# High parts ahead of low ones, P5's sum on P1's weight tile, and a new order of the last product, in a decoder trunk on one core

## The chip, the core and the metric

The kernel runs on one core of one Trainium2 chip. A core has five engines with a queue each, executed in order: TensorE (PE, matmuls), VectorE (DVE), ScalarE (ACT), GpSimd (POOL) and SyncE (SP). SP here only issues loads; POOL issues the loads that add to what lies in a tile. Data come from the chip's memory into on-chip tiles; products are accumulated in PSUM banks and read from there by DVE and ACT. The metric is the device time of one execution in microseconds (us).

## The reference

A trunk of two layers on 512 tokens of width 1024, all in float32. Layer 0 mixes tokens with a gated linear recurrence, layer 1 with a spatial gate; each mixer stands between two feed-forward blocks of width 2816 that count half.

```python
def swiglu(x, w_in, w_out):
    g, u = jnp.split(x @ w_in, 2, axis=-1)
    return (jax.nn.silu(g) * u) @ w_out
...
    for i in range(DEPTH):
        h = h + 0.5 * swiglu(rms_norm(h, ffn1_norm[i]), ffn1_w_in[i], ffn1_w_out[i])
        hn = rms_norm(h, mix_norm[i])
        ...
        h = h + m          # m: recurrent mixer (i = 0) or spatial gating mixer (i = 1)
        h = h + 0.5 * swiglu(rms_norm(h, ffn2_norm[i]), ffn2_w_in[i], ffn2_w_out[i])
    return rms_norm(h, final_norm)
```

## The kernel before

**Products.** A float32 operand is split into a high part (rounded, by ACT, line 96) and a low part (the rest, by DVE, line 87 or 93); a product is three matmuls, left high by weight high, left low by weight high, left high by weight low (lines 362 to 364). The splits of weights are called whi and wlo, those of activations hi and lo.

**Seven products instead of eight.** `seven` cuts both operands of a matrix product into 2 x 2 blocks and forms it from seven products, P1 P2 P5 P6 P3 P7 Q4, by the scheme of Strassen and Winograd. Their left operands are blocks or sums of blocks of the activations (A11, A12, S1, S2, S4, S3, A22, in that order); S1 = A21 - A22, S2 = S1 - A11, S4 = S2 + A12 and S3 = -S2 - A22. Their right operands are weight blocks: B11 for P1, B21 for P2, B11 + B12 for P5, B11 + B12 + B22 for P6, the same and B21 for Q4, B22 for P3, and B12 + B22 for P7 (signs left aside). P1, P6, P7 and Q4 gather in bank pair A (Q4 of an out product in Q), P5 and P3 in C, P2 in B. Each product is cut into two parts, ci = 0 and 1, by rows of the weights. A product's `posts` read its bank when its second part is through: in an out product they add the bank to the trunk X (`upd`, line 93 by its helper, "x<-A" in the profile), where P6's must have read bank A before P7 writes it again.

**Steps.** All products stand in one list `subs`, 550 entries, one for a product's part; an entry's twelve or so matmuls are one step. The loop at the end of `trunk` goes through them in order and emits for step i: waiting accumulating loads that are due (`run_pending`); hooks "pre"; the split of the weights of step i + 3 (`Sub.split`) after the DVE sum of the next one (`Sub.add`); hooks "mid" and "rest"; plain loads into weight tiles that are free (`load_more`, SP's queue); the matmuls; hooks "end"; the product's posts; hooks "late". Each engine executes its instructions in this order. There are 8 weight tiles as loaded ("raw") and 4 each of whi and wlo.

**Sums of weight blocks** are made in three ways. `Raw(plus=...)` loads one block plainly, and two steps later issues a load on POOL's queue that adds the second (line 136; `pending`). `Sub.then` issues such an adding load right after a split has read the tile. `Sub.tile` has DVE add two tiles (line 87, "raw<-raw,raw"), and `tile_then` then adds a further block to the second tile. A seven with `own=True` loads B11 a second time for P5 and gives P5 and P7 sums of the first kind; with `own=False`, P5's sum is one of DVE's, and P7 goes on with the tile of that sum. P6 adds B22 by DVE and then B21 by a load for Q4. Where P6 comes four steps or more behind P5 (`far`: the recurrent mixer's out product, and part 0 of the spatial one's), P5's split is followed by the load of B22 instead.

**Stages.** A feed-forward block is three times a group of columns of w_in and the matching rows of w_out: first a "pair" of column tiles by plain products (`pair_plain`, line 727) and a chunk of four tiles by `seven` (`chunk`), then two such chunks twice (lines of `FF_PARTS`); each time the out product follows (`out_blocks`, own=True). Chunks have own=False, but one of the spatial mixer is own. The recurrent out product has the order P1 P5 P2 for each part, P6 P3 for each, then P7 and Q4; its left operands are split `lead` = 2 steps ahead. The last out product has an order of its own, `FinalNorm.ORDER`, and its P3 is held back to the end with both parts together (`joined`).

**Turning activations.** A left operand's blocks are transposed by PE into a PSUM bank (`Group.turn`, line 264, "e"), from which ACT and DVE take them, split or as they are (`Group.take`, `Group.direct`). `direct` runs in the opening, where the first norm's blocks are turned, and at the norms between blocks (`BlockNorm`). In the opening the first pair's own turns (`left_blocks`, from `post` in `pair_plain`) stand at a lag of 4 steps. The first chunk takes bank pair B from the two `aux` banks, in which the turned blocks also lie; its P2's post adds B to c (line 87, "c<-c,B"). ACT squares the quarters of X there for the next norm (`squares`).

Of the kernel before, what the change touches and what calls it, by code (L numbers as in the profile page):

```python
# [13 lines left out]
P = 128  # L14
# [38 lines left out]
def trunk(ctx: ExitStack, tc: tile.TileContext, a: dict, out: bass.AP):  # L53
# [57 lines left out]
    class Raw:  # L111
# [1 line left out]

        halves = False

        def __init__(self, src, shape, plus=None):
            self.src, self.shape, self.plus, self.uses, self.done = src, shape, plus, 0, 0

        def turn(self):
            self.uses += 1  # L120
# [2 lines left out]
        def load(self):  # L123
            _, k, c = self.shape
            t = rawp.tile([P, 1024], F32, tag="raw", name=nm("raw"))
            self.v = t[:, : k * c].rearrange("p (k c) -> p k c", k=k)
            live.add(self)
            self.fetch()
            if self.plus is not None:
                pending.append((now[0] + 2, self))  # L130

        def fetch(self):
            nc.sync.dma_start(out=self.v, in_=self.src)
# [68 lines left out]

    raws = []

    def raw_of(src, shape, plus=None):
        raws.append(Raw(src, shape, plus))
        return raws[-1]

    subs = []
# [35 lines left out]
    class Group:  # L245
# [39 lines left out]
        def direct(self, name, ps, gains):  # L285

            hi, lo = self.hl[name] = slot(F32R, "hi")[:, : self.n * H], slot(F32R, "lo")[:, : self.n * H]
            for q, g in enumerate(gains):
                c = slice(q * H, (q + 1) * H)
                act(hi[:, c], ps[:, c], AF.Copy, scale=g)  # L290
                stt(lo[:, c], ps[:, c], g, f32(hi[:, c]), ALU.mult, ALU.subtract)

        def stage(self, n, name, src, gains=None, parts=True, where=None, direct=0):
# [40 lines left out]
    def seven(block, cuts, left, w, posts, order=None, own=False, apart=False, joined=None, spare=bank):  # L334

        bk, raw, held = {}, {}, []
        banks = dict(BANK, Q4=("Q", True)) if apart else BANK

        def mm_of(prod, ci):
            name, fresh = banks[prod]
            pairs = cuts[ci]

            def mm(sub):
                if fresh and ci == 0:
                    for s in range(2):  # L350
                        bk[name, s] = (spare if name == "B" else bank)(name)[:, :w]
                if prod == joined and ci == 0:
                    held.extend((sub, q, i) for q, i in enumerate(pairs))
                    return
                for s in range(2):
                    ps = bk[name, s]
                    k = {} if fresh else dict(skip_group_check=True)
                    for sb, q, i in (held if prod == joined else []) + [(sub, q, i) for q, i in enumerate(pairs)]:
                        zh, zl = left(prod, i, s)
                        wh, wl = sb.hi[:, q, :], sb.lo[:, q, :]  # L360
                        end = i == cuts[-1][-1]
                        nc.tensor.matmul(ps, zh, wh, start=fresh and i == 0, stop=False, **k)  # L362
                        nc.tensor.matmul(ps, zl, wh, start=False, stop=False, **k)  # L363
                        nc.tensor.matmul(ps, zh, wl, start=False, stop=end, **k)  # L364
                    if ci == len(cuts) - 1 and prod in posts:
                        posts[prod](s, ps)
            return mm

        order = order or [(p, ci) for p in ORDER for ci in range(len(cuts))]

        def far(ci):
            return own and order.index(("P6", ci)) - order.index(("P5", ci)) >= 4

        for prod, ci in order:
            def new(k, n, plus=None):
                b = lambda k, n: block(k, n, cuts[ci])
                return raw_of(b(k, n), [P, len(cuts[ci]), w], plus and b(*plus))

            tile = then = tile_then = None
            if prod == "P1":  # L380
                r = raw[11, ci] = new(0, 0)
            elif prod == "P2":
                r = new(1, 0)
            elif prod == "P5":
                if own:
                    raw[11, ci] = new(0, 0, (0, 1))
                    if far(ci):
                        then = block(1, 1, cuts[ci])
                else:
                    tile = raw[12, ci] = new(0, 1)  # L390
                    tile_then = block(1, 1, cuts[ci])
                r = raw[11, ci]
            elif prod == "P6" and far(ci):
                r, then = raw[11, ci], block(1, 0, cuts[ci])
            elif prod == "P6":
                r, tile, then = raw[11, ci], new(1, 1), block(1, 0, cuts[ci])
                raw[22, ci] = tile
            elif prod == "P3":
                r = new(1, 1) if far(ci) else raw[22, ci]
            elif prod == "P7":  # L400
                r = new(0, 1, (1, 1)) if own else raw[12, ci]
            else:
                r = raw[11, ci]
            subs.append(Sub(r, mm_of(prod, ci), None, tile, then, tile_then))
        return order

# [149 lines left out]
                hook(n + 4, "pre", lambda: self.take(1))  # L556


    def out_blocks(w, k0, groups, scale, norm=None, order=None, own=False):

        n = [g for g in groups]
        cuts, bases, i, r = [], {}, 0, k0
# [57 lines left out]
        for i, (prod, ci) in enumerate(order):  # L620
            if prod in ("P3", "P6", "P7", "Q4"):
                lead = 6 if ends and prod == "P3" else 4 if isinstance(norm, TileNorm) and prod in ("P7", "Q4") else 3 if 1 in n else 2
                hook(at0 + i - lead, "mid", lambda ci=ci, name=LEFT[prod]: gs[ci].parts(name))
        return gs

# [27 lines left out]
        return left_of(lambda: S.z)  # L653


    def chunk(w_in, f0, nt, group, spare=bank):

        w = nt * P
        c1, c2, c3, c5, ht = {}, {}, {}, {}, {}

        def rt(t):
            return S.rt[:, t : t + 1]

        def new(d, s, name):
            d[s] = slot(name=name)[:, :w]
            return d[s]

        def p1(s, ps):
            act(new(c1, s, "c1"), ps, AF.Copy)

        def p2(s, ps):
            tt(c1[s], c1[s], ps, ALU.add)
            hook(now[0] + 1, "mid", lambda: act(c1[s], c1[s], AF.Silu, scale=rt(s)))

        def p5(s, ps):
            act(new(c5, s, "c5"), ps, AF.Copy)

        def p6(s, ps):
            act(new(c2, s, "c2"), ps, AF.Copy)

        def p3(s, ps):
            tt(c2[s], ps, c2[s], ALU.subtract)
            stt(c2[s], c2[s], rt(s), c1[s], ALU.mult, ALU.mult)
            ht[s] = c2[s]
            if s == 1:
                left_blocks(group, ht, 0)

        def p7(s, ps):
            act(new(c3, s, "c3"), ps, AF.Copy)
            hook(now[0] + 1, "mid", lambda: tt(c5[s], c5[s], c3[s], ALU.subtract))  # L690

        def q4(s, ps):
            s4 = slot(name="s4")[:, :w]
            act(s4, ps, AF.Silu, scale=rt(2 + s))
            stt(c5[s], c5[s], rt(2 + s), s4, ALU.mult, ALU.mult)
            ht[2 + s] = c5[s]
            if s == 1:
                left_blocks(group, ht, 1)

        seven(in_block(w_in, lambda n: n * DFF + f0 * P, w), [[0, 1], [2, 3]], x_left(), w,  # L700
              dict(P1=p1, P2=p2, P5=p5, P6=p6, P3=p3, P7=p7, Q4=q4), spare=spare)

    def pair_plain(w_in, f0, group, first=False):

# [31 lines left out]
        def post(half):  # L736
            for s in range(2):
                ps, t = st[half, s], 2 * half + s
                if t not in ht:
                    silu(half, s)  # L740
                o = slot(name="h")[:, :w]
                stt(o, ps[:, w:], S.rt[:, t : t + 1], ht[t], ALU.mult, ALU.mult)
                ht[t] = o
            left_blocks(group, ht, half, 4 if first else 2)

        at0 = len(subs)
        for i, (half, left) in enumerate(((0, "A12"), (0, "A11"), (1, "A22"), (1, "A21"))):
# [27 lines left out]
    def ffn(w_in, w_out, norm):  # L775
        f0 = 0
        for i, sizes in enumerate(FF_PARTS):
            groups, p0 = [], f0
            for n in sizes:
# [3 lines left out]
                    f0 += 2  # L783
                else:
                    groups.append(Group(n // 2))
                    chunk(w_in, f0, n, groups[-1], aux if len(subs) == 8 else bank)
                    f0 += n
            gs = out_blocks(w_out, p0, [g.n for g in groups], 0.5, norm if i == len(FF_PARTS) - 1 else None, own=True)
            gs.update(enumerate(groups))
# [2 lines left out]
    class FinalNorm:  # L792

        ORDER = [(p, ci) for p in ("P1", "P2", "P5", "P6", "P7", "Q4", "P3") for ci in range(2)]

        def __init__(self):
            self.gain, self.q, self.m, self.s = {}, {}, {}, {}
# [95 lines left out]
    def recurrent(w_in, w_out, norm):  # L895
# [132 lines left out]
        for i, at in enumerate(((11, 12, 15), (13, 14, 16))):  # L1028
            for fn, n in zip((groups[i].s2, groups[i].s4, groups[i].s3), at):
                hook(y0 + n, "pre", fn)  # L1030

        def y_post(c, ps):
            ym[c] = ps
# [31 lines left out]
        order = [(p, ci) for ci in range(2) for p in ("P1", "P5", "P2")]  # L1065
        order += [(p, ci) for ci in range(2) for p in ("P6", "P3")]
        order += [(p, ci) for p in ("P7", "Q4") for ci in range(2)]
        gs = out_blocks(w_out, 0, [2, 2], 1.0, norm, order, own=True)
        gs.update(enumerate(groups))


# [358 lines left out]
                         (4, "rest", lambda: (value(0, "A21"), value(1, "A21")))):  # L1430
        hook(n, phase, fn)
    squares(4, "rest", "A11")
    squares(4, "rest", "A12")
    squares(5, "rest", "A22")
    squares(5, "rest", "A21")
    rstd(6, (0, "rest"), (0, "rest"), (1, "pre"))
    first.rest(1, None)
    hook(20, "end", vec_rest_t)
# [50 lines left out]
```

## Time and profile before

| what | value |
|---|---|
| median of 3 runs | 1652.9 us (1652.57 to 1654.43) |
| the profiled execution | 1653.5 us |
| its span in the trace | 1651.7 us |
| matmuls (PE) | 7475 |
| granted TensorE clock, mean | 0.995 |
| moved by plain loads (q1) and by POOL's (q0) | 182.74 MB and 87.63 MB |
| their share of the 16 DMA engines' span | 35.8% and 31.7% |

The span runs from the first instruction to the last in the trace; 1.8 us of the profiled execution lie outside it. A group in the profile is named by line, engine, operation and tiles, with tile numbers left out: "A<-whi,hi" is a matmul into a bank called A from a weight's high part and an activation's high part. A wait names the instruction that came last before the waiting one could start. The page's list of DMA issues gives for each kind of load its bytes and its median time from issue to landing: the plain 512 KB loads of w_out take 5.4 us in the median, those of w_in 4.5.

### The profile page before, as it was taken

To read this page: it belongs to the slowest core of one execution; us is meant where nothing else is said; L and a number is where in the kernel's file an instruction comes from. 1 tells how busy PE (TensorE), PEld (TensorE's weight loads), DVE (VectorE), ACT (ScalarE), POOL (GpSimd) and SP (SyncE) were. 2 spreads that over 40 slices of the span, in tenths; PEclk is the share of its full clock that TensorE was granted. 3 is DMA by queue.
4 is the path that set the end of the run, shared out by engine and by line. 5 is a ranking of instruction groups with operands and counts; after the bars stand their busy time and mean duration, and the time that the engine had idled before them with its cause. 6 is when DMAs were issued, how large, how long until landed. Compare 5 with 4: busy or idle time off the path is not lost.

```text
span 1651.7 us, 20816 instructions
## 1 busy us (share of the span) xinstructions
PE 1621.3 (98%) x7475; PEld 1334.7 (81%) x7475; DVE 1361.2 (82%) x1821; ACT 1033.6 (63%) x1501; POOL 214.1 (13%) x194
## 2 busy tenths in 40 slices
PE   9899999999999999999999999999999999999997
PEld 7688888888878888888888888888788888888885
DVE  6898897887798797877987978778866888879777
ACT  6656556667867556556775565566774865665655
POOL 1111111200010111111101111112101011121110
PEclk9999999999999999999999999999999999999999
DMA  5667966853373876876838768769864557686683
GB/s 211 148 167 177 217 156 165 210 146 102 90 179 92 183 184 174 207 169 161 203 86 191 170 171 208 175 163 217 193 165 104 152 119 187 166 207 168 157 205 79
DMA packets 161560, 273.54 MB, mean 166 GB/s; under 512 B 11328, under 2 KB 37552, under 8 KB 161456
## 3 DMA queue, kind: packets, MB, share of 16 engines
q1 hardware_dynamic: 113856, 182.74, 35.8%
q0 software_dynamic: 45808, 87.63, 31.7%
q10 hardware_dynamic: 1792, 1.84, 0.4%
q8 instruction: 59, 0.97, 0.2%
q14 instruction: 45, 0.37, 0.1%
HBM read 270.07 MB, written 2.10 MB: 165 GB/s over the span
## 4 chain that ended last, share of the span: by engine, by line
PE 87%; DVE 6%; ACT 4%; issue 1%; DMA 1%; SPq 0%; ACTq 0%; DVEq 0%
PE A L362 13%; PE A L363 13%; PE A L364 13%; PE C L363 7%; PE C L364 7%; PE C L362 7%; PE p L727 4%; PE e L264 3%; PE B L362 3%; PE B L364 3%; PE B L363 3%; DVE wlo L87 2%; PE Q L364 1%; PE Q L362 1%; PE Q L363 1%
## 5 line engine op out<-in xcount | busy, mean ns | idle before, releaser
L96 ACT ACTIVATE whi<-raw 128x1024 fp32r<-128x1024 f32 (+1 forms) x530 | 547.0, 1033 | 416.4 <-PE A L363 114.5
L87 DVE TENSOR_TENSOR wlo<-raw,whi 128x1024 fp32r<-128x1024 f32 (+1 forms) x531 | 631.1, 1191 | 207.1 <-ACT whi L96 205.7
L362 PE MATMUL A<-whi,hi 128*128 128x512 f32 x984 | 392.1, 398 | 4.4 <-DVE x L93 4.4
L364 PE MATMUL A<-wlo,hi 128*128 128x512 f32 x984 | 384.9, 391 | 0.0
L363 PE MATMUL A<-whi,lo 128*128 128x512 f32 x984 | 384.5, 391 | 0.2 <-DVE lo L87 0.2
L362 PEld LDWEIGHTS A<-whi,hi 128*128 128x128 f32 x984 | 185.2, 188 | 41.3 <-issue 4.8
L362 PE MATMUL C<-whi,hi 128*128 128x512 f32 x544 | 213.8, 393 | 4.4 <-ACT hi L96 4.4
L364 PEld LDWEIGHTS A<-wlo,hi 128*128 128x128 f32 x984 | 185.1, 188 | 40.3
L363 PEld LDWEIGHTS A<-whi,lo 128*128 128x128 f32 x984 | 185.5, 189 | 37.8 <-DVE lo L87 1.2
L363 PE MATMUL C<-whi,lo 128*128 128x512 f32 x544 | 214.0, 393 | 1.8 <-DVE lo L87 1.5
L364 PE MATMUL C<-wlo,hi 128*128 128x512 f32 x544 | 213.2, 392 | 1.2 <-DVE wlo L87 1.2
L136 POOL DMA_DIRECT2D raw<-in_ffn_w_in_dram x80 | 96.4, 1205 | 750.4 <-DVE raw L87 558.6
L136 POOL DMA_DIRECT2D raw<-in_ffn_w_out_dram x72 | 83.0, 1156 | 390.3 <-DVE wlo L87 155.0
L87 DVE TENSOR_TENSOR raw<-raw,raw 128x1024 f32<-128x1024 f32 (+1 forms) x107 | 128.2, 1199 | 0.5
L87 DVE TENSOR_TENSOR lo<-a,hi 128x512 fp32r<-128x512 f32 (+1 forms) x188 | 122.6, 659 | 3.7 <-ACT hi L96 3.1
L362 PEld LDWEIGHTS C<-whi,hi 128*128 128x128 f32 x544 | 103.0, 189 | 26.9 <-ACT hi L96 5.5
L363 PEld LDWEIGHTS C<-whi,lo 128*128 128x128 f32 x544 | 102.9, 189 | 26.3 <-DVE lo L87 5.1
L364 PEld LDWEIGHTS C<-wlo,hi 128*128 128x128 f32 x544 | 102.9, 189 | 23.0 <-DVE wlo L87 1.7
L96 ACT ACTIVATE hi<-a 128x512 fp32r<-128x512 f32 (+1 forms) x188 | 112.5, 600 | 13.0 <-DVE a L87 10.8
L96 ACT ACTIVATE c<-A 128x512 f32<-128x512 f32 x126 | 74.1, 594 | 57.0 <-PE A L364 56.4
L362 PE MATMUL B<-whi,hi 128*128 128x512 f32 x272 | 109.0, 401 | 0.0
L364 PE MATMUL B<-wlo,hi 128*128 128x512 f32 x272 | 106.5, 391 | 0.6 <-DVE wlo L87 0.6
(170 smaller groups left out, 2202.9 us busy)
## 6 DMA issues: line engine op xcount, KB each, us to landing
raw<-in_ffn_w_in_dram SPq DMA_DIRECT2D x160, 512.0 KB, 4.5
raw<-in_ffn_w_out_dram SPq DMA_DIRECT2D x100, 512.0 KB, 5.4
raw<-in_ffn_w_in_dram POOLq DMA_DIRECT2D x80, 512.0 KB, 7.5
raw<-in_ffn_w_out_dram POOLq DMA_DIRECT2D x60, 512.0 KB, 7.7
raw<-in_sg_w_in_dram SPq DMA_DIRECT2D x18, 512.0 KB, 5.1
raw<-in_rec_w_in_dram SPq DMA_DIRECT2D x16, 512.0 KB, 3.9
raw<-in_ffn_w_in_dram SPq DMA_DIRECT2D x30, 256.0 KB, 4.0
raw<-in_ffn_w_out_dram SPq DMA_DIRECT2D x20, 256.0 KB, 4.8
```

The source lines that it names most:

```text
L87: nc.vector.tensor_tensor(out=o, in0=x, in1=y, op=op)
L96: nc.scalar.activation(out=o, in_=x, func=f, **k)
L136: nc.gpsimd.dma_start(out=self.v, in_=src, accum_op=ALU.add)
L264: nc.tensor.transpose(ps[:, o : o + P], src(q, s), ident)
L362: nc.tensor.matmul(ps, zh, wh, start=fresh and i == 0, stop=False, **k)
L363: nc.tensor.matmul(ps, zl, wh, start=False, stop=False, **k)
L364: nc.tensor.matmul(ps, zh, wl, start=False, stop=end, **k)
L727: nc.tensor.matmul(bank_of(half, s), z, (sub.lo if m == 2 else sub.hi)[:, q, :], start=left[2] == "2" and (h, q, m) == (0, 0, 0), stop=lef ...
```

## The change

- `direct` first has ACT write both high parts from the bank, then DVE both low parts.
- In an own seven whose P5 comes four steps or more behind P1 (`again`), P5 has no tile of its own: after P1's split a load adds B12 to P1's tile. This holds for the out products of all feed-forward blocks and the spatial mixer's own chunk.
- The first chunk of all is own (it alone has its B in the `aux` banks, as before).
- The first pair's turns come one step later (lag 5).
- The squares of the quarter A12 come one step later, those of A22 and A21 too.
- Where P6 is far, P7's waiting sum is due 6 - ci steps after its plain load instead of 2.
- The recurrent out product splits the left operand of P3's first part three steps ahead instead of two.
- The last out product has the order P1 P2 P6 P5 P7 Q4 P3. Its P6 has tiles of its own: B11, and B12 with B22 added by a waiting load; DVE adds the two, P7 goes on with the second, Q4 with the first, and P3 loads B22 anew.

```diff
-        def __init__(self, src, shape, plus=None):
-            self.src, self.shape, self.plus, self.uses, self.done = src, shape, plus, 0, 0
+        def __init__(self, src, shape, plus=None, wait=2):
+            self.src, self.shape, self.plus, self.wait, self.uses, self.done = src, shape, plus, wait, 0, 0
 
         def turn(self):
             self.uses += 1
...
             if self.plus is not None:
-                pending.append((now[0] + 2, self))
+                pending.append((now[0] + self.wait, self))
+                pending.sort(key=lambda p: p[0])
 
         def fetch(self):
             nc.sync.dma_start(out=self.v, in_=self.src)
...
-    def raw_of(src, shape, plus=None):
-        raws.append(Raw(src, shape, plus))
+    def raw_of(src, shape, *plus):
+        raws.append(Raw(src, shape, *plus))
         return raws[-1]
 
     subs = []
...
             hi, lo = self.hl[name] = slot(F32R, "hi")[:, : self.n * H], slot(F32R, "lo")[:, : self.n * H]
-            for q, g in enumerate(gains):
-                c = slice(q * H, (q + 1) * H)
+            cs = [(slice(q * H, (q + 1) * H), g) for q, g in enumerate(gains)]
+            for c, g in cs:
                 act(hi[:, c], ps[:, c], AF.Copy, scale=g)
+            for c, g in cs:
                 stt(lo[:, c], ps[:, c], g, f32(hi[:, c]), ALU.mult, ALU.subtract)
 
         def stage(self, n, name, src, gains=None, parts=True, where=None, direct=0):
...
+        def again(ci):
+            return own and order.index(("P5", ci)) - order.index(("P1", ci)) >= 4
         for prod, ci in order:
-            def new(k, n, plus=None):
+            def new(k, n, plus=None, wait=2):
                 b = lambda k, n: block(k, n, cuts[ci])
-                return raw_of(b(k, n), [P, len(cuts[ci]), w], plus and b(*plus))
+                return raw_of(b(k, n), [P, len(cuts[ci]), w], plus and b(*plus), wait)
 
             tile = then = tile_then = None
             if prod == "P1":
                 r = raw[11, ci] = new(0, 0)
+                if again(ci):
+                    then = block(0, 1, cuts[ci])
             elif prod == "P2":
                 r = new(1, 0)
             elif prod == "P5":
-                if own:
+                if again(ci):
+                    pass
+                elif own:
                     raw[11, ci] = new(0, 0, (0, 1))
                     if far(ci):
                         then = block(1, 1, cuts[ci])
...
                 r = raw[11, ci]
+            elif prod == "P6" and joined:
+                r, tile, then = new(0, 0), new(0, 1, (1, 1)), block(1, 0, cuts[ci])
+                raw[6, ci], raw[12, ci] = r, tile
             elif prod == "P6" and far(ci):
                 r, then = raw[11, ci], block(1, 0, cuts[ci])
             elif prod == "P6":
                 r, tile, then = raw[11, ci], new(1, 1), block(1, 0, cuts[ci])
                 raw[22, ci] = tile
             elif prod == "P3":
-                r = new(1, 1) if far(ci) else raw[22, ci]
+                r = new(1, 1) if far(ci) or joined else raw[22, ci]
             elif prod == "P7":
-                r = new(0, 1, (1, 1)) if own else raw[12, ci]
+                r = raw[12, ci] if joined or not own else new(0, 1, (1, 1), 6 - ci if far(ci) else 2)
             else:
-                r = raw[11, ci]
+                r = raw[6 if joined else 11, ci]
             subs.append(Sub(r, mm_of(prod, ci), None, tile, then, tile_then))
         return order
...
-    def out_blocks(w, k0, groups, scale, norm=None, order=None, own=False):
+    def out_blocks(w, k0, groups, scale, norm=None, order=None, own=False, soon={}):
 
         n = [g for g in groups]
         cuts, bases, i, r = [], {}, 0, k0
...
                 lead = 6 if ends and prod == "P3" else 4 if isinstance(norm, TileNorm) and prod in ("P7", "Q4") else 3 if 1 in n else 2
+                lead = soon.get((prod, ci), lead)
                 hook(at0 + i - lead, "mid", lambda ci=ci, name=LEFT[prod]: gs[ci].parts(name))
         return gs
...
-    def chunk(w_in, f0, nt, group, spare=bank):
+    def chunk(w_in, f0, nt, group, first=False):
 
         w = nt * P
         c1, c2, c3, c5, ht = {}, {}, {}, {}, {}
...
         seven(in_block(w_in, lambda n: n * DFF + f0 * P, w), [[0, 1], [2, 3]], x_left(), w,
-              dict(P1=p1, P2=p2, P5=p5, P6=p6, P3=p3, P7=p7, Q4=q4), spare=spare)
+              dict(P1=p1, P2=p2, P5=p5, P6=p6, P3=p3, P7=p7, Q4=q4), own=first, spare=aux if first else bank)
 
     def pair_plain(w_in, f0, group, first=False):
...
                 ht[t] = o
-            left_blocks(group, ht, half, 4 if first else 2)
+            left_blocks(group, ht, half, 5 if first else 2)
 
         at0 = len(subs)
         for i, (half, left) in enumerate(((0, "A12"), (0, "A11"), (1, "A22"), (1, "A21"))):
...
                     groups.append(Group(n // 2))
-                    chunk(w_in, f0, n, groups[-1], aux if len(subs) == 8 else bank)
+                    chunk(w_in, f0, n, groups[-1], len(subs) == 8)
                     f0 += n
             gs = out_blocks(w_out, p0, [g.n for g in groups], 0.5, norm if i == len(FF_PARTS) - 1 else None, own=True)
             gs.update(enumerate(groups))
...
-        ORDER = [(p, ci) for p in ("P1", "P2", "P5", "P6", "P7", "Q4", "P3") for ci in range(2)]
+        ORDER = [(p, ci) for p in ("P1", "P2", "P6", "P5", "P7", "Q4", "P3") for ci in range(2)]
 
         def __init__(self):
             self.gain, self.q, self.m, self.s = {}, {}, {}, {}
...
                 hook(y0 + n, "pre", fn)
+        soon = {("P3", 0): 3}
 
         def y_post(c, ps):
             ym[c] = ps
...
         order += [(p, ci) for p in ("P7", "Q4") for ci in range(2)]
-        gs = out_blocks(w_out, 0, [2, 2], 1.0, norm, order, own=True)
+        gs = out_blocks(w_out, 0, [2, 2], 1.0, norm, order, own=True, soon=soon)
         gs.update(enumerate(groups))
...
     squares(4, "rest", "A11")
-    squares(4, "rest", "A12")
-    squares(5, "rest", "A22")
-    squares(5, "rest", "A21")
+    squares(5, "rest", "A12")
+    squares(6, "rest", "A22")
+    squares(6, "rest", "A21")
     rstd(6, (0, "rest"), (0, "rest"), (1, "pre"))
```

## The prediction

> **What bounds the kernel.** First the head of the page: busy time by engine, and the chain that ended last.
>
> ```profile
> span 1651.7 us, 20816 instructions
> ...
> PE 1621.3 (98%) x7475; PEld 1334.7 (81%) x7475; DVE 1361.2 (82%) x1821; ACT 1033.6 (63%) x1501; POOL 214.1 (13%) x194
> ...
> PE 87%; DVE 6%; ACT 4%; issue 1%; DMA 1%; SPq 0%; ACTq 0%; DVEq 0%
> ```
>
> TensorE is busy 98% of the span, and no product is added or removed, so only its idle 30 us (1651.7 - 1621.3) and the places where it runs at half rate can be won. Then the busy time by stretch (us, then PE, PEld, DVE, ACT, POOL with counts, granted clock, DMA share, GB/s) shows where the idle time lies:
>
> ```profile
> 0.00:60.00 60.00, 49.02 (x208) 36.92 (x209) 44.78 (x75) 39.68 (x75) 10.20 (x19) 0.94 0.59 179
> 370.00:500.00 130.00, 126.53 (x595) 104.79 (x594) 107.39 (x147) 96.18 (x144) 9.69 (x8) 0.99 0.51 126
> 1170.00:1300.00 130.00, 127.51 (x617) 105.18 (x616) 94.52 (x154) 83.99 (x134) 13.30 (x11) 1.00 0.61 149
> 1600.00:1652.00 52.00, 40.10 (x173) 32.37 (x171) 40.89 (x66) 27.13 (x47) 4.81 (x4) 0.92 0.39 93
> ```
>
> The opening lacks 11.0 us of PE, the recurrent stage 3.5, the spatial stage 2.5, the end 11.9 (7.2 of them after the last matmul). Third, the waits (total us, times, longest) name what ended them:
>
> ```profile
> POOL raw L136 <- DMA raw<-in_ffn_w_out_dram: 162.6, 16, 36.3
> ...
> ACT hi L96 <- DVE lo L93: 14.4, 16, 2.5
> ...
> ACT whi L96 <- DMA raw<-in_rec_w_out_dram: 7.9, 1, 7.9
> ...
> PE e L264 <- DVE c L87: 6.3, 1, 6.3
> ...
> PE C L362 <- ACT hi L96: 4.4, 3, 2.6
> PE A L362 <- DVE x L93: 4.4, 1, 4.4
> ```
>
> Last, the timelines of PE and of ACT at these places (start, length, idle before and its releaser):
>
> ```profile
> 56.22 0.69 PE L264 MATMUL e<-ident,h 128*128 128x128 f32 x2 [6.33 <-DVE c L87]
> ...
> 1626.31 0.47 PE L362 MATMUL A<-whi,hi 128*128 128x512 f32 x1 [4.39 <-DVE x L93]
> ```
>
> ```profile
> 476.84 1.06 ACT L96 ACTIVATE whi<-raw 128x1024 fp32r<-128x1024 f32 x1 [7.94 <-DMA raw<-in_rec_w_out_dram]
> 477.80 0.61 ACT L96 ACTIVATE hi<-a 128x512 fp32r<-128x512 f32 x1
> ```
>
> Matmuls start 0.227 us apart, a step of twelve takes 2.72 us. After the long stalls some eight or nine start 0.43 us apart, so such a stall costs about 9 x 0.2 = 1.6 to 2 us more.
>
> **The change, part by part** (gains positive).
>
> *Opening: +6.2 (4.5 to 8).* PE stalls 0.37, 0.58 and 1.40 us ahead of P1, P2 and P5 of the first chunk, then 6.3 for transposes whose two spare banks B still holds until DVE's sum c<-c,B (55.49) has read them, then runs at half rate: P5's second half starts at 56.56 and P6 at 61.43. Four edits act here. High parts first: ACT's second hi (0.47) no longer waits for DVE's first lo (0.48); eight of the 16 such waits lie here, about 1 us of ACT. Two squares of 0.6 instead of four go ahead of the chunk's splits: 1.2 us. P5's two sums on DVE (1.14 each) go to DMA: DVE reaches c<-c,B at 55.49 - 2.3 = 53.2, and its first half ends some 0.65 later, 53.9. The transposes stand behind P5's second half instead of ahead of it, so that half (2.72) fills part of the wait. With the first three stalls mostly gone P5 starts near 44 instead of 45.44; its second half waits for its low parts on DVE (near 48.7) some 1.3; it ends near 51.5; PE then waits about 2.4 for the transposes (53.9, 0.35 long), and P6 starts at 54.25: 61.43 - 54.25 = 7.2. Does half rate follow a 2.4 us stall? Rows on both sides: stalls of 1.40 (45.66) and of 1.2 + 0.5 (1196) were not followed by it, 2.75 + 1.11 (475.5) was. 2.4 lies nearer to the latter; I take half of 2: 7.2 - 1.0 = 6.2. The squares put back and the later sums of squares have one to two steps until their norm is read, on an ACT that is 66% busy: nothing.
>
> The Trainium skill ("TensorE: Matmul & The Clock Gate", Part 1) has the clock halve after an idle window of about 3.4 us and return after as long a busy one. The stall of 2.75 + 1.11, which contains no single idle stretch that long, was followed by half rate here, so the trace is harsher than the page; by the page's figure the opening would give 7.2, as in the second rival below.
>
> *Recurrent out stage: +5.5 (4 to 6).* PE waits 2.75 and 1.11 at 475.5, then loses about 2 at half rate: 5.9. ACT waited 7.94 for P6's accumulating load, and P3's high part stood behind that wait. The load was issued at 466.98 and took 9.75, because P7's, ahead of it on POOL's queue, waited for its own plain load until 465.69. P7's wait of 6 - ci steps puts it behind P6's, which can issue when P5's split has ended (464.5); at the 90% duration of such loads here, 9.6, it would land at 474, at the median 7.4 at 472: ACT's wait falls to 3 to 5 us, and P3's high part, one step earlier (0.6 of ACT), is ahead of it. P7's load then is first needed ten us later.
>
> *Spatial chunk: +2.4 (1 to 3.3).* Three stalls (1.47, 1.7, 0.45 = 3.6) at 1191 to 1201, where ACT is busy without a break and twice waits 1.3 for lo inside a pair of hi. 2 x 1.3 comes off ACT. In return DVE's first lo waits for both hi (0.47 later), and ACT's next copy from the same bank for both lo (up to 0.48 more): some 0.5 per pair comes back, so 2.4 of 3.6, with all of it and a third of it as bounds. The other six pairs lie where PE loses nothing.
>
> That wait is what the Trainium skill ("PSUM — Partial Sum Buffer", section "PSUM bank collisions raise a hardware error") asks for: two engines may not touch one bank at a time, reads included. The 16 waits of 14.4 us agree. By it alone, with ACT as the bound and nothing lost elsewhere, this part would still give 2.4.
>
> *End: +4.9 (3.5 to 6).* P7's first matmul waits 4.39 (4.55 over its spacing) for P6's update x<-A (1625.48), as both use bank A with nothing between; then about 1.6 at half rate: 6.1. With P5 (bank C, two steps, 5.4 us) between P6 and P7, P6's update comes some 7 us earlier in DVE's queue, before P7 starts at 1621.8: all of it goes. DVE is busy without a break from 1616.65 to 1628.5, so that PE comes ahead of it in the tail; P7, Q4 and the norm's Newton steps then wait for DVE some 1.2 more: 6.1 - 1.2.
>
> *P5 on P1's tile: -3 (-12 to 0).* In eleven ffn out stages and the spatial chunk it takes two plain loads each off SP's queue, 24 in all; POOL's sums stay as many (two more in the first chunk), but P5's is now issued after P1's split instead of as soon as a tile of its own has landed, three steps later. Each of these stages thus issues P7(0), P1(0), P7(1), P1(1) within two steps, in this order. Between the end of P1's low part and the start of P5's high part lie 9.55 and 8.84 us (pair stages), 9.5 and 7.8 (stages with "p"). The rows:
>
> ```profile
> raw<-in_ffn_w_out_dram POOLq DMA_DIRECT2D x60, 512.0 KB, 7.7
> ```
>
> A median of 7.7 fits; the longest, 11.9, does not, and landings of loads issued back to back are 2.5 apart alone and 4.1 beside plain loads. For the stage at 194 to 217 I get a landing of P1(1)'s sum at 200.5 to 203.6; P5(1)'s high part started at 200.36, its low part at 202.92, on a DVE without a break whose next deadline (S2's low part) has 0.6 us to spare. So PE loses landing + 1.03 - 202.92 - 0.6 = landing - 202.5: 0 to 1.1, mean 0.4. Seven ffn stages of pairs: 2.8; in the four with "p" (landing 570.9 to 572.5, wanted at 572.1) 0 to 0.4 each. I take 3 of up to 12 as most landings fall inside. SP's queue, shorter by 24 loads, can only help; this is the upper bound of 0.
>
> Sum: 6.2 + 5.5 + 2.4 + 4.9 - 3.0 = 16.0. The profiled execution's span becomes 1635.7; with the 1.8 us outside the span (1653.5 - 1651.7) 1637.5. The median shown, 1652.9, lies 0.6 below the profiled execution: **1636.9, say 1637**.
>
> **Rivals.** *Half gained:* PE, freed of these stalls, catches up with DVE (82% busy, without a break at the opening and at the end). For: DVE ended two of the four large stalls. Against: the sums leave DVE, and between the stages it has room. Opening 4.5, end 3.5, recurrent 4, spatial 1, sums -4: 9.0, 1643.9.
>
> *The sums come in time everywhere:* price 0, opening without half rate, 7.2: 20.0, 1632.9. For: 24 fewer loads beside them. Against: the bunching on one queue.
>
> *Slower: late sums stall each out stage.* For: P1's sum goes behind P7's on a queue that is served in order; P7's waited for its own plain load up to 36 us in before (162.6 in 16 waits), and a sum behind it would wait as well. If the landing comes 3 us after the end of the room, ACT and DVE stand at P5's split, PE loses 2.5 twice in each of the eight pair stages (the spatial chunk with them) and 1.5 twice in four "p" stages: 40 + 12 = 52; less 19.0 from the others, +33, 1686. It decides from a mean loss of 0.8 per sum (24 x 0.8 = 19). Against: where P7's load lands late in before, its tile was freed late; 24 fewer loads free tiles sooner.
>
> *It doesn't do what it says:* P6's update is not what holds P7, or DVE's queue delays it all the same (1618.5 wanted, 1621.8 allowed: 3.3 to spare). Then the end gives 0: 11.1, 1641.8.
>
> **How the numbers follow.** Forecast 0.43, all in time 0.13, end unchanged 0.08, half gained 0.2, slower 0.16. The forecast's own range adds the terms' ends where they go together half way: 1632 to 1642. For 8 in 10 the range reaches from all in time (opening at 8: 1631) over half gained to a loss of 7 by the sums beside it: 1650. Within 0.2% (3.3 us, about what a measurement of this kernel can tell from no change) falls only a mixed case: 0.02 of half gained and 0.03 of slower. Faster 0.43 + 0.13 + 0.08 + 0.18 = 0.82, same 0.05, slower 0.13.
>
> **What would show it.** The row "PE e <- DVE c" falls from 6.3 to below 3; "PE A L362 <- DVE x L93" is gone and P7 follows P5 at full rate; ACT's wait for in_rec_w_out falls below 5 and "PE C <- ACT hi" with it; "ACT hi <- DVE lo" falls from 14.4 to near 0; SP's loads of in_ffn_w_out number 24 fewer. Wrong: new waits "ACT whi <- DMA raw<-in_ffn_w_out_dram" of over 1 us each and PE idle in C at P5 of each out stage; or a granted clock below 0.94 in the first 60 us.

## The result, and the profile after

| | us |
|---|---|
| before, median of 6 runs beside the changed kernel | 1653.55 (1652.38 to 1654.43) |
| changed kernel, median of 6 runs | 1666.96 (1661.08 to 2907.88) |
| ratio | 1.0074, 95% interval 1.0053 to 1.0095 |
| changed kernel, second set of 4 runs | 1669.06 (1666.21 to 1673.40), ratio 1.0096 (1.0078 to 1.0113) |

The change makes the kernel slower by 13 to 16 us; the forecast was 16 us faster. One of the first six executions, the profiled one, ran at a granted clock of 0.72 and took 2907.88 us, so the ratio leaves it out, and the profile shown here is that of the second set, of an execution of 1669.04 us. Lines stand 1 to 16 lower in the file: 137 for 136 (POOL's adding load), 265 for 264, 365 to 367 for 362 to 364 (the three matmuls).

First the head of the page and the chain of waits:

```profile
span 1667.2 us, 20783 instructions
...
PE 1627.5 (98%) x7475; PEld 1337.2 (80%) x7475; DVE 1357.2 (81%) x1819; ACT 1029.2 (62%) x1501; POOL 218.8 (13%) x196
...
PE 74%; DVE 10%; DMA 8%; issue 3%; ACT 3%; POOL 1%; SPq 0%; POOLq 0%; DVEq 0%; ACTq 0%
```

Neither DVE nor ACT has more to do. PE's idle time has grown from 30.4 to 39.7 us, and its busy time, in which matmuls at half rate count, by 6.2. And the chain, in which DMA had 1%, now goes 8% through loads, 7 of them of in_ffn_w_out, and 10% through DVE. Then the waits (total us, times, longest):

```profile
POOL raw L137 <- DMA raw<-in_ffn_w_out_dram: 150.2, 18, 15.4
...
ACT whi L96 <- DMA raw<-in_ffn_w_out_dram: 54.8, 12, 6.2
...
PE A L366 <- DVE lo L87: 20.4, 13, 2.5
...
PE e L265 <- DVE c L87: 1.3, 1, 1.3
```

The four waits that the change aimed at are gone or small: the transposes wait 1.3 us for c<-c,B instead of 6.3, and P7's wait for x<-A, ACT's for P6's load in the recurrent stage and "ACT hi <- DVE lo" are no longer among the waits listed. In their place stand two groups that the profile of before does not have at this size: ACT's high part of a weight waits 54.8 us, twelve times, for loads of in_ffn_w_out, and PE waits 20.4 us, thirteen times, at P6 for a low part (0.2 in before). A feed-forward out stage is called a pair stage below, or a "p" stage where the columns of `pair_plain` belong to it; there the first part of each product has half the rows. The busy time by stretch (columns as in the prediction) shows the opening won, and a pair stage (188 to 231) and a "p" one (562 to 599) that lack 1.9 and 2.7 us of PE. In before, the stretches in which these two lie lack 0.0, 0.1 and 0.4 us in all:

```profile
110.00:340.00 230.00, 230.00 (x1046) 190.17 (x1045) 197.00 (x263) 139.62 (x180) 35.66 (x32) 1.00 0.78 185
500.00:580.00 80.00, 79.90 (x370) 65.65 (x369) 66.28 (x98) 52.12 (x84) 9.91 (x9) 1.00 0.57 130
580.00:1170.00 590.00, 589.62 (x2692) 486.06 (x2692) 497.12 (x600) 363.79 (x504) 84.14 (x71) 1.00 0.75 179
```

Changed kernel:

```profile
0.00:60.00 60.00, 55.55 (x250) 42.92 (x251) 45.36 (x78) 44.83 (x85) 12.71 (x21) 1.00 0.79 222
188.00:231.00 43.00, 41.08 (x185) 33.61 (x185) 39.03 (x57) 21.52 (x27) 2.41 (x2) 1.00 0.64 156
562.00:599.00 37.00, 34.27 (x146) 27.25 (x145) 32.22 (x47) 18.66 (x27) 3.25 (x3) 0.95 0.64 164
```

One such loss, followed through three engines, in the pair stage at 189 to 230. POOL's adding loads first (start, time to issue, idle before and its releaser). In before, where this stage starts 5.5 us later, P5's two sums come first, and P7's some 13 us behind them:

```profile
181.84 1.20 POOL L136 DMA_DIRECT2D raw<-in_ffn_w_out_dram  x1 [9.78 <-DMA raw<-in_ffn_w_out_dram]
184.36 1.20 POOL L136 DMA_DIRECT2D raw<-in_ffn_w_out_dram  x1 [1.31 <-DVE c L87]
197.46 2.48 POOL L136 DMA_DIRECT2D raw<-in_ffn_w_out_dram  x2 [11.90 <-DMA raw<-in_ffn_w_out_dram]
```

P5's second sum landed at 195.93 there and was first read at 200.36, so that it had 4.4 us to spare. In the changed kernel:

```profile
181.78 2.44 POOL L137 DMA_DIRECT2D raw<-in_ffn_w_out_dram  x2 [15.22 <-DMA raw<-in_ffn_w_out_dram]
184.82 1.20 POOL L137 DMA_DIRECT2D raw<-in_ffn_w_out_dram  x1 [0.61 <-DMA raw<-in_ffn_w_out_dram]
186.33 1.20 POOL L137 DMA_DIRECT2D raw<-in_ffn_w_out_dram  x1 [0.30 <-DVE wlo L87]
```

These four are P7(0), P1(0), P7(1), P1(1). By the trace they land at 188.24, 191.37, 194.19 and 198.94: in order, 3.1, 2.8 and 4.75 us apart. The last one, P5's second tile, takes 12.6 us from issue to landing. On the clock of before (5.5 later) it is issued 7.5 us later than there and lands 8.5 us later, which is more than the 4.4 to spare. Then ACT and PE:

```profile
199.04 1.06 ACT L96 ACTIVATE whi<-raw 128x1024 fp32r<-128x1024 f32 x1 [5.85 <-DMA raw<-in_ffn_w_out_dram]
...
203.89 1.06 ACT L96 ACTIVATE whi<-raw 128x1024 fp32r<-128x1024 f32 x1 [2.31 <-DVE raw L87]
```

```profile
206.27 0.39 PE L365 MATMUL A<-whi,hi 128*128 128x512 f32 x1
208.58 0.50 PE L366 MATMUL A<-whi,lo 128*128 128x512 f32 x1 [1.92 <-DVE lo L87]
```

ACT waits 5.85 us for that landing. DVE's low part of the tile follows it at 200.14, and everything queued behind it on DVE is late, down to P6's left operand, whose low part starts at 207.84: PE has done the first matmul of P6 and stands. P5's own matmuls, whose weights were split three steps ahead, do not wait here; the delay comes out at the next product.

### The profile page after: what moved, and what is told of

It is laid out like the page before. It is cut to its first block, busy times and chain, and to the rows that moved or that the text cites. A ratio compares the mean times of both kernels' runs of the same rounds, so it can differ in the third digit from the quotient of the medians.

```text
span 2905.9 us, 20783 instructions
## 1 busy us (share of the span) xinstructions
PE 2897.4 (100%) x7475; PEld 1763.9 (61%) x7475; DVE 1400.9 (48%) x1819; ACT 1050.9 (36%) x1501; POOL 216.2 (7%) x196
## 4 chain that ended last, share of the span: by engine, by line
PE 100%; DVE 0%; ACT 0%; issue 0%
PE A L365 14%; PE A L367 14%; PE A L366 14%; PE C L367 8%; PE C L365 8%; PE C L366 8%; PE p L742 6%; PE B L366 4%; PE e L265 4%; PE B L365 4%; PE B L367 4%; PE r L225 2%; PE r L224 2%; PE r L223 2%; PE Q L365 1%; PE Q L366 1%
## 5 line engine op out<-in xcount | busy, mean ns | idle before, releaser
L365 PE MATMUL A<-whi,hi 128*128 128x512 f32 x984 | 603.4, 613 | 0.0
L367 PE MATMUL A<-wlo,hi 128*128 128x512 f32 x984 | 592.7, 602 | 0.0
L366 PE MATMUL A<-whi,lo 128*128 128x512 f32 x984 | 592.1, 602 | 0.0
L367 PEld LDWEIGHTS A<-wlo,hi 128*128 128x128 f32 x984 | 235.7, 240 | 163.7 <-issue 111.0
L365 PE MATMUL C<-whi,hi 128*128 128x512 f32 x544 | 328.3, 604 | 0.0
L367 PE MATMUL C<-wlo,hi 128*128 128x512 f32 x544 | 327.4, 602 | 0.0
L366 PE MATMUL C<-whi,lo 128*128 128x512 f32 x544 | 327.2, 602 | 0.0
L365 PE MATMUL B<-whi,hi 128*128 128x512 f32 x272 | 168.1, 618 | 0.0
L366 PE MATMUL B<-whi,lo 128*128 128x512 f32 x272 | 164.5, 605 | 0.0
L367 PE MATMUL B<-wlo,hi 128*128 128x512 f32 x272 | 164.4, 604 | 0.0
```

## The experiments

All times below are medians; before was 1653.5 to 1654.7 beside them. The first four kernels repeat the changed one, take the suspected part out, put it in alone, and move one transfer. "Theories" are those of the first expectation below.

**The changed kernel again.**

> The changed kernel again, for a profile at full clock (the first one was taken at a clock of 0.72). Theory 1 (P5's sums, bunched with P7's on POOL's queue, land late and stall the out stages; the other edits gain about 19): 1661 to 1667, with PE idle at P5 of the feed-forward out stages and ACT's whi waiting for loads of in_ffn_w_out there, some 30 us in all; the opening, recurrent, spatial and end stages gain as forecast. Theory 2 (the sums come in time, but the other edits gain nothing or lose): the out stages as before, and the stalls at the four places still there. Theory 3 (clock): no new wait, but a lower granted clock or a wider spacing of the matmuls.

Measured: 1669.06, 2 above the range, with the waits above. Theory 1 holds in kind, though PE stands at P6 and not at P5. Theory 2 had no gain at the four places, theory 3 no new wait.

**Without P5 on P1's tile.**

```diff
         def again(ci):
-            return own and order.index(("P5", ci)) - order.index(("P1", ci)) >= 4
+            return False
```

> The change without its second part: P5 loads a tile of its own again and its sum waits two steps, everything else as changed. Theory 1: 1635 (1630 to 1640). Theory 2: 1655 or more, as the changed kernel. Theory 3: as the changed kernel within 5.

Measured: 1637.01 (1636.61 to 1641.46), ratio 0.9906 (0.9891 to 0.9921). The other parts gain 16.5 together, and this part costs 32. (The longest execution is the profiled one: its last out stage is 5.6 us longer, because P6's sum on DVE waits there for an adding load that took 11.4 us.)

**P5 on P1's tile alone**, in the kernel before:

```diff
+        def again(ci):
+            return own and order.index(("P5", ci)) - order.index(("P1", ci)) >= 4
...
                 r = raw[11, ci] = new(0, 0)
+                if again(ci):
+                    then = block(0, 1, cuts[ci])
...
-                if own:
+                if again(ci):
+                    pass
+                elif own:
```

> The kernel before with the second part alone: P5 on P1's tile. Theory 1: 1680 to 1690. Theory 2: 1650 to 1656. Theory 3: not above 1660.

Measured: 1684.97 (1683.95 to 1686.32), ratio 1.0190 (1.0175 to 1.0205): 31.5 slower. With and without the other parts the cost is the same.

**P7's sum later.** What is it that makes the sums late: that P1's are issued after its split, or that P7's are ahead of them?

```diff
-                r = raw[12, ci] if joined or not own else new(0, 1, (1, 1), 6 - ci if far(ci) else 2)
+                r = raw[12, ci] if joined or not own else new(0, 1, (1, 1), 6 - ci if far(ci) else 5)
```

> The changed kernel with P7's waiting sum due 5 steps after its plain load instead of 2 in the stages where P6 is near, so that it is issued behind both of P5's sums on POOL's queue instead of ahead of them. Theory 1, if it is P7's sums ahead in the queue: 1640 to 1648; theory 1, if P1's late issue alone is enough: 1658 or more. Theories 2 and 3: no change from the changed kernel, 1661 to 1667.

Measured: 1636.54 (1636.28 to 1637.15), ratio 0.9897 (0.9880 to 0.9914). The whole cost is gone, where a part of it was expected to stay. The same two stages lack 0.0 and 0.2 us of PE now:

```profile
186.00:226.00 40.00, 40.00 (x182) 33.09 (x181) 38.36 (x56) 21.21 (x27) 4.25 (x4) 1.00 0.72 171
556.00:587.00 31.00, 30.84 (x139) 24.90 (x138) 29.49 (x44) 17.99 (x26) 2.87 (x3) 1.00 0.79 202
```

In the first of them, 2.2 us earlier on the clock, POOL's queue is now

```profile
180.24 1.20 POOL L137 DMA_DIRECT2D raw<-in_ffn_w_out_dram  x1 [15.84 <-DVE wlo L87]
184.16 3.68 POOL L137 DMA_DIRECT2D raw<-in_ffn_w_out_dram  x3 [2.73 <-DVE wlo L87]
```

with P1(0), P1(1), P7(0), P7(1). P1's two are issued at the same points of the stage as in the changed kernel (180.24 and 184.16, against 182.5 and 186.33 less 2.2) and land at 185.96 and 189.91, 5.7 us after issue each; P7's two, right behind, take 9.4 and 13.5, and nobody waits for them. No wait of ACT for in_ffn_w_out is left in the list. So it was neither the late issue nor the number of loads in flight, but the place in the queue.

**P7's sum one step and two steps later**, to see how much room is needed (2 above replaced by 3, and by 4):

> The changed kernel with P7's waiting sum due after 3 steps instead of 2 in the stages where P6 is near: on POOL's queue one of P7's sums stands between P1's two, the other behind them, so that P1's first sum has none of P7's ahead and its second has one. If a sum ahead costs its turn on the queue (3 to 4 us) and the room is short by some 2: 1638 to 1645. If only the room in which all four are issued counts (load on the DMA engines): 1655 to 1665.

Measured: 1636.05 (1635.44 to 1636.50), 2 us below the first expectation. POOL's order is P1(0), P7(0), P1(1), P7(1):

```profile
179.19 2.44 POOL L137 DMA_DIRECT2D raw<-in_ffn_w_out_dram  x2 [15.84 <-DVE wlo L87]
183.12 2.44 POOL L137 DMA_DIRECT2D raw<-in_ffn_w_out_dram  x2 [1.49 <-DVE wlo L87]
```

They land at 185.47, 188.50, 191.80 and 196.04. One sum ahead costs P1(1) 3 us (8.7 from issue to landing instead of 5.7), and the room takes that: ACT's waits for in_ffn_w_out come to 5.9 us in three, and PE has no wait from it.

> The same with 4 steps: both of P7's sums right behind P1's two. If the place on the queue decides: 1636.5, as with 5 steps. If the distance of P7's sums from P1's decides: 1640 or more.

Measured: 1636.52 (1636.09 to 1636.90), the same as with 5 steps: the distance does not matter.

All three, 1636.05 to 1636.54, stand beside 1637.01 without P5 on P1's tile, and the intervals of their ratios overlap with its. So even in the right order of loads this part, with its 24 plain loads fewer, gains nothing that these runs can tell.

The next four undo one of the other parts each, in the version with 5 steps (1636.54). They ran in another set, beside a before of 1653.79 instead of 1653.51. Where stages are compared, the first 20 us are left out: they hang on the first loads and differ by up to 1.3 us between executions.

**direct in its old order.**

```diff
-            cs = [(slice(q * H, (q + 1) * H), g) for q, g in enumerate(gains)]
-            for c, g in cs:
+            for q, g in enumerate(gains):
+                c = slice(q * H, (q + 1) * H)
                 act(hi[:, c], ps[:, c], AF.Copy, scale=g)
-            for c, g in cs:
                 stt(lo[:, c], ps[:, c], g, f32(hi[:, c]), ALU.mult, ALU.subtract)
```

> The version with P7's sum five steps after its load (1636.5), with the old order in direct (high, low, high, low). Additive theory: what the part gained comes back, 2.4 in the spatial chunk and up to 1 in the opening: 1639 to 1640. Rival (ACT has slack at those places once the other parts are in): 1636 to 1637.

Measured: 1642.40 (1641.98 to 1642.78): 5.9 comes back, more than expected. By the starts of PE's matmuls the opening is 3.1 longer, the recurrent out stage 0.8 and the spatial chunk 2.6. "ACT hi <- DVE lo" is back with 13.6 us in 16 waits.

**The opening's three other edits undone** (first chunk not own, lag 4, the squares at 4, 5, 5):

> The same version (1636.5) with the opening's three other edits undone: first chunk not own, first pair's turns at lag 4, squares at their old steps. The opening's 7.9 us between the two traces come back less the share of direct: 1642.5 to 1644.5. Rival (direct did most of it): 1638 or less.

Measured: 1641.38 (1640.83 to 1641.49): 4.8 comes back, less than expected, because direct had more: the opening is 4.9 longer by the starts of PE's matmuls, and with direct's 3.1 that makes 8.0, near the 8.3 between before and the version with 5 steps. PE waits 5.8 for c<-c,B again.

**The recurrent stage's two edits undone** (P7's sum after 2 steps where P6 is far, no `soon`):

> The same version (1636.5) with P7's waiting sum due after 2 steps where P6 is far, and P3's left operand two steps ahead in the recurrent out product, as before. By the traces (the stage is 2.6 shorter than before) 1639; by the forecast of 5.5, 1642. Rival (another edit did it): 1636.5.

Measured: 1639.74 (1639.49 to 1640.22): 3.2 (3.3 in the stage itself), near the reading of the traces, not the forecast's 5.5.

```profile
ACT whi L96 <- DMA raw<-in_rec_w_out_dram: 8.0, 1, 8.0
...
PE C L365 <- ACT hi L96: 2.7, 1, 2.7
```

The first was 7.9 in before, and the second is the longest of the three waits of its kind there, 2.6.

**The last product in its old order.**

```diff
-        ORDER = [(p, ci) for p in ("P1", "P2", "P6", "P5", "P7", "Q4", "P3") for ci in range(2)]
+        ORDER = [(p, ci) for p in ("P1", "P2", "P5", "P6", "P7", "Q4", "P3") for ci in range(2)]
```

> The same version (1636.5) with the last out product in its old order P1 P2 P5 P6 P7 Q4 P3, its new tiles kept. By the forecast 1641.4, by the traces (last matmul 5.3 earlier, tail 1.8 longer) 1640; PE again waits for x<-A ahead of P7. Rival (the new tiles did it): 1636.5.

Measured: 1642.99 (1641.65 to 1643.69): 6.4 comes back in the medians. Between the traces the last out stage with the tail behind it is 5.7 longer than in the version with 5 steps, and 2.1 longer than in before: in the changed kernel the old order is slower than it was there. The wait that the new order removes is back:

```profile
PE A L365 <- DVE x L93: 5.0, 1, 5.0
```

The four come to 5.9 + 4.8 + 3.2 + 6.4 = 20.3, against 17.0 for all (1653.5 - 1636.5), so they do not add. By the traces the surplus lies in two places: in the recurrent out stage, where direct and the two edits give 0.8 + 3.3 singly but 2.6 together, and at the end, 5.7 against 3.5.

**Two more operands early in the recurrent stage.**

```diff
-        soon = {("P3", 0): 3}
+        soon = {("P3", 0): 3, ("P6", 1): 3, ("P7", 0): 3}
```

> The version with 5 steps (1636.5) with the left operands of P6's second and P7's first part split three steps ahead in the recurrent out product too, as PE still waits 0.93 for a low part at P6 and 0.94 for a high part at P7 there. If the hooks' place causes the two waits: 1634.5 to 1635.5. If they come from ACT's wait for the load of P6's tile (2.47): 1636.5 or more.

Measured: 1635.84 (1635.08 to 1636.37). P6's wait of 0.93 is gone, P7's has grown from 0.94 to 1.32; the 0.7 gained lies within what these runs can tell. Inconclusive.

## Why the prediction was wrong

**What bounds the kernel, and the four places: right.** The four parts other than P5's sums were forecast at 19.0 together and gave 16.5 to 17.0 (without P5 on P1's tile, and with 5 steps). By the starts of PE's matmuls in the version with 5 steps against before:

| part | forecast (bounds) | measured in the trace | undone singly, in the trace |
|---|---|---|---|
| opening, up to the first out stage, without the first 20 us | 6.2 (4.5 to 8) | 8.3 (64.8 to 56.5 long) | 4.9, and 3.1 of direct |
| recurrent out stage | 5.5 (4 to 6) | 2.6 (47.13 to 44.50 long) | 3.3, and 0.8 of direct |
| spatial chunk | 2.4 (1 to 3.3) | 2.7 (44.33 to 41.65 long) | 2.6 of direct |
| end, tail with it | 4.9 (3.5 to 6) | 3.5 | 5.7 |

Stalls here and below are counted beyond the usual distance between two starts, as in the prediction; the lists of waits show 0.1 to 0.3 less. In the opening, which gained a little more than its upper bound, the transposes' remaining stall was 1.5 us instead of 2.4, another of 1.2 follows one step on, and no half rate came after them: the half of 2 us taken for it was not needed. At the end, which gained what the lower bound said, the tail behind the last matmul grew by 1.8, from 7.2 to 9.0, where 1.2 had been allowed. The recurrent term was mis-sized below its bounds. ACT's wait fell from 7.9 to 2.5, better than the 3 to 5 forecast, but PE came on the next ones: 0.93 at P6, 0.94 at P7 and 1.1 at the norm's transposes, none of which is in the working. The stage's 5.9 was priced as though nothing stood behind the stall.

**The step that failed: P5 on P1's tile, "-3 (-12 to 0)".** It cost 32, more than two and a half times its own lower bound. For the stage that it worked out, the order of the four sums, the room and the formula (landing - 202.5) were right. What was wrong is the landing. On the clock of before, in which this stage starts 5.5 later, P1(1)'s sum landed at 198.94 + 5.5 = 204.4, not at 200.5 to 203.6; the formula then gives 1.9, and the stage measured 2.2. In the "p" stage the landing was 575.3 (572.2 + 3.1), not 570.9 to 572.5, and the stage lost 4.5, two stalls of 1.0 and 2.0 and eight matmuls at half rate behind them. The step knew spacings of 2.5 to 4.1 us and let the sums be mostly inside; four served in order took 3.1 + 2.8 + 4.75 behind the first's own 6.5. From the first landing (188.24 + 5.5 = 193.7) three of its own spacings would have reached 201.2 to 206.0, past the 203.6 at which its range ended. And the median of 7.7 us that it leaned on is no measure of a sum in line: in before it mixes P6's loads, which mostly stand alone (5.7 to 6.4 for 512 KB), with sums such as P5's second one, which took 9.1 to 11.6 in nine of the eleven stages. In the changed kernel P1's second sum took 10.1 to 12.9 in all eleven. Then the step took the mean of a quantity that is cut off at zero, so that landings 0.8 to 4.4 us later than its range, in the two stages that it worked out, cost 2.2 and 4.5 us, and all twelve stages 32 instead of 3.

Stage by stage the loss against the version with 5 steps is, in us: 3.4, 4.5, 4.4 and 3.9 in the four "p" stages; 2.2, 2.6, 4.0, 0.6, 2.0, 1.5 and 1.1 in the seven of pairs; 3.5 in the spatial chunk; together 33.7 (32.2 between the spans, as the changed kernel's execution was 1.3 ahead when the first loads were in). The "p" stages, priced at 0 to 0.4, are the worst: their first parts have half the rows and half the time, while the second parts' sums are as long as anywhere.

**The rival that came true** is the slower one. Its mechanism, a sum of P1 that goes behind P7's on a queue served in order, is what the runs show, and its point of decision (0.8 us per sum) was passed: 32 / 24 = 1.3. Its price, 52, was too high: it had both sums of a stage late. The second held ACT up for 4.5 to 6.2 us in nine of the eleven feed-forward stages, the first in three of them, for 1.0 to 2.1. Its argument that P7's sum would hold up the queue until its own tile has landed does not explain the pair stages, where P1's sums were issued in time; in the "p" stage at 563 it made the last one 1 us later.

**What it said would show it wrong** did: "ACT whi <- DMA raw<-in_ffn_w_out" at 4.6 us each (54.8 / 12). PE's idle time was expected in C at P5; nearly all of it is in A at P6. SP's plain loads did fall by 24, but 22 of them are loads of in_ffn_w_out and 2 those of the spatial chunk.

## What to carry to other kernels

A transfer that moves from "as soon as a tile is there" to "after something has read it" loses its slack; before pricing it, write down what stands ahead of it on its queue and add the service times, since on POOL's queue here the order of issue was the order of landing. Where a cost is zero up to a point and then grows, take it from the late end of the landing times, and multiply by the number of places. And a change that is slower as a whole can hold parts that gain: one step's delay for the transfers that nobody is waiting for turned 0.7 to 1.0% slower into 1.1% faster.

## What the runs showed of the hardware

In the changed kernel, adding loads of 512 KB with none ahead of them on POOL's queue took 5.7 to 8.9 us from issue to landing (45 of 163); the three of these with no plain load in flight beside them took 5.7 to 5.9. One issued while another was under way landed 2.1 to 6.9 us after it, 3.2 in the median, and 2.5 in the median of the 24 beside no plain load. Loads behind do not show as a cost to one that is ahead: with three behind it, it took 5.7 to 8.5 us. The Trainium skill ("DMA: Bandwidth & Descriptors", section "SWDGE vs HWDGE vs iDMA") has accumulating DMAs on GpSimd's path alone and one queue for it; the traces agree, as all 175 adding loads of weights land in order of issue.

In the changed kernel half rate (seven or eight starts 0.43 us apart) followed single stalls of PE of 2.12, 2.25 and 2.75 us (91, 694 and 1200 us) and three pairs, of 0.4 to 1.0 and, some 5 us later, of 1.94 to 1.99 (579, 921 and 1401), but not the single stalls of 2.08 (206) and 1.82 (1036). The Trainium skill ("TensorE: Matmul & The Clock Gate", Part 1) gives an idle window of about 3.4 us that runs on its own clock. A stall of 2.12 us cannot hold such a window whole, wherever the window starts, so that here less idle time was enough, and the measurement decides. Whether the stretch that counts runs on its own clock, which might explain 2.12 against 2.08, no run here shows.
